# Storing a hybrid decoder's output by whole 128-partition banks, the last one in two column halves

## The chip, the core and the metric

The kernel runs on one core of a Trainium2 chip, as one program. The metric is the device time of one execution in microseconds (us). On the core, TensorE (PE in the profile) multiplies matrices into PSUM, the accumulator memory; VectorE (DVE) and ScalarE (ACT) do elementwise work; GpSimd (POOL) does small things; SyncE (SP) only issues transfers. Transfers between SBUF, the on-chip memory of 128 partitions, and DRAM run on 16 DMA engines. SP and ACT each have a queue from which these engines are fed (q1 and q10 in the profile).

## The reference

Two layers over a sequence of 256 tokens of 1024 numbers. Each layer adds half a SwiGLU block, a token mixer (a diagonal state-space mixer in layer 0, block attention in layer 1), and another half of a SwiGLU block:

```python
def swiglu(h, w_gate, w_up, w_down):
    return (jax.nn.silu(h @ w_gate) * (h @ w_up)) @ w_down
...
    for layer in range(DEPTH):
        h = h + MACARON_WEIGHT * swiglu(rms_norm(h, ffn_norm[layer, 0]), ...)
        hn = rms_norm(h, mix_norm[layer])
        ...
        h = h + MACARON_WEIGHT * swiglu(rms_norm(h, ffn_norm[layer, 1]), ...)
    return h
```

All is float32. D_MODEL is 1024, D_FF is 2816, and the output is 256 x 1024 floats, 1 MB.

## The kernel before

The residual h stays in SBUF all the time, as one tile of 128 partitions x 2 x 1024. `h[t]` is its half for tokens 128 t to 128 t + 127. Tokens are interleaved over the partitions: partition p of half t holds token 128 t + 4 (p mod 32) + p // 32. So 32 neighbouring partitions hold every fourth token, and `rows(t, s, n)` gives the DRAM list for the partitions 32 s to 32 s + 31: 32 entries, 4 rows of D = 1024 floats apart, of 512 floats each.

Weights arrive as 1 MB tiles through the SP queue. They are split into a high and a low part (`Stream.split`), and each product is made of three matmuls (`mm3`: high x high, high x low, low x high), for accuracy. All six phases run one behind the other with TensorE as the common thread. The order of the instructions on every engine is the order of the program's text.

The change touches the end of the last phase, f11, a SwiGLU block in `ffn_w`. Its second product, act @ w_down, collects in four PSUM banks `acc[2 * t + n]`: t is the half of the tokens, n the half of the 1024 columns; a bank has 128 partitions x 512 floats. `boundary` (line 362) closes every phase. For the last one (`nxt` is None) the order of the banks is (0, 0), (0, 1), (1, 0), (1, 1), called banks 0 to 3 here. Its `parts` are the last three of the 22 steps of the contraction: for each bank, three calls of `bank_mm` (line 406) with three matmuls of 512 columns each (lines 386 to 388). The parts of banks 0 and 1 but the last come first; then, bank by bank:

- the last part of banks 0 and 1, or all three parts of banks 2 and 3, on TensorE;
- `finish` (line 358): h = 0.5 * acc + h for the bank, one VectorE instruction of 512 columns (line 360);
- `store` (line 414): four transfers of 32 partitions x 512 floats, 64 KB each, the first and third from SP, the second and fourth from ACT (line 418).

Nothing else follows on TensorE and VectorE. On SP, the last weight tile has been issued long before; on ACT the last activation stands ahead of the first store. The program ends when the last transfer has landed, with waits, drains and clearing of semaphores on all engines (line 1428 in the profile).

Of the kernel before, what the change touches and what calls it, by code (L numbers as in the profile page):

```python
# [13 lines left out]
OP = mybir.AluOpType  # L14
AX = mybir.AxisListType

D = 1024
# [98 lines left out]
def trunk_kernel(ctx: ExitStack, tc, x, ffn_norm, ffn_w_gate, ffn_w_up, ffn_w_down, mix_norm,  # L116
                 s5_w_in, s5_a_re, s5_a_im, s5_log_dt, s5_b_re, s5_b_im, s5_c_re, s5_c_im, s5_d,
                 s5_w_glu, s5_w_out, moba_w_qkv, moba_q_norm, moba_k_norm, moba_w_out,
                 consts, out, phases=("f00", "s5", "f01", "f10", "moba", "f11")):
    nc = tc.nc  # L120
# [10 lines left out]
    def psM():  # L131
        return pp.tile([128, 512], F32, name="pM", tag="M", bufs=2)
# [4 lines left out]
    def psA(i):  # L137
        return pp.tile([128, 512], F32, name=f"pA{i}", tag=f"A{i}", bufs=1)

    mm = nc.tensor.matmul  # L140
# [10 lines left out]
    where = {}  # L151
# [74 lines left out]
    def warm(func):  # L226

        w = sp.tile([128, 1], F32, name="warm", tag="warm", bufs=1)
        nc.scalar.activation(w, ones[:, 0:1], func)
# [10 lines left out]
    h = [h2[:, t, :] for t in range(2)]  # L240

    def rows(t, s, n):

        tiles = [[128 * D, 2]] if t is None else []
        return [((t or 0) * 128 + s) * D + n * 512, [[4 * D, 32]] + tiles + [[1, 512]]]
# [66 lines left out]
    def prep(t, n, ph, sq=True):  # L312

        if (ph, "x") not in X:
            X.clear()
            X[ph, "x"] = True
            X["h"], X["l"] = home(XP[0], ph)
        hh = h[t][:, n * 512:(n + 1) * 512]
        ps = psR()
        pv = ps.rearrange("p (k c) -> p k c", c=128)  # L320
        for k in range(4):
            nc.tensor.transpose(pv[:, k, :], hh[:, k * 128:(k + 1) * 128], ident)  # L322
        xh, xl = (X[p][:, n * 4:n * 4 + 4, t * 128:t * 128 + 128] for p in "hl")
        nc.scalar.activation(xh, pv, AF.Copy)
        nc.vector.tensor_tensor(xl, pv, xh.bitcast(F32), op=OP.subtract)
        if sq:
            squares(t, n)
# [30 lines left out]
    def finish(t, n, acc, scale):  # L358
        hh = h[t][:, n * 512:(n + 1) * 512]
        nc.vector.scalar_tensor_tensor(hh, acc, scale, hh, op0=OP.mult, op1=OP.add)  # L360

    def boundary(nxt, parts, acc, scale, mid=None):

        if nxt is not None and nxt[0] == "f":
            order = [(0, 0), (1, 0), (0, 1), (1, 1)]
        else:
            order = [(0, 0), (0, 1), (1, 0), (1, 1)]
        for i in range(2):
            for part in parts[:-1]:
                part(*order[i])  # L370
            if mid is not None and i == 0:
                mid()
        for i, (t, n) in enumerate(order):
            for part in parts[-1:] if i < 2 else parts:
                part(t, n)
            finish(t, n, acc[2 * t + n], scale)
            if nxt is None:
                store(t, n)
            elif i:
                prep(*order[i - 1], nxt)  # L380

    def entry_hooks(ph):
        return {2: [lambda: prep(1, 1, ph)]}

    def mm3(o, xh, xl, wh, wl, start, stop):
        mm(o, xh, wh, start=start, stop=False)  # L386
        mm(o, xh, wl, start=False, stop=False)  # L387
        mm(o, xl, wh, start=False, stop=stop)  # L388

    def product(o, t, uA, uB, hooks, pumps=(1, 5)):  # L390

# [11 lines left out]
                if t == 1:  # L403
                    st.release(u, (k % 4) // 2)

    def bank_mm(acc, t, n, lh, ll, u, kks, first, last):

        for kk in kks:
            wh, wl = st.get(u, kk)
            c = slice(n * 512, n * 512 + 512)  # L410
            mm3(acc[2 * t + n], lh[:, kk, t * 128:t * 128 + 128], ll[:, kk, t * 128:t * 128 + 128],
                wh[:, c], wl[:, c], first and kk == kks[0], last and kk == kks[-1])

    def store(t, n):
        hh = h[t][:, n * 512:(n + 1) * 512]
        for s in range(4):
            off, ap = rows(t, s, n)
            (nc.sync, nc.scalar)[s % 2].dma_start(bass.AP(tensor=out.tensor, offset=out.offset + off, ap=ap),
                                                  hh[s * 32:s * 32 + 32])


    def ffn(tag, nxt, hooks, fill):
# [67 lines left out]
        def dn(j, f):  # L490
            u = where[tag, "d", j]
            for t in range(2):
                for n in range(2):
                    if j == 0 and f == 0:
                        acc[2 * t + n] = psA(2 * t + n)
                    bank_mm(acc, t, n, *AT[j], u, [f], j == 0 and f == 0, False)
                    fill(0.7)
                if t == 1:
                    st.release(u, f)
                st.pump()  # L500
# [21 lines left out]
    def ffn_w(tag, nxt, entry):  # L522

        V = nc.vector
        acc = [None] * 4
        AT = {}

        def gu(j, f, hooks):
            us = [where[tag, "g", j, a] for a in range(2)]
            ps = psM()  # L530
            for k in range(8):
                for fn in hooks.get(k, ()):
                    fn()
                wh, wl = st.get(us[k // 4], (k % 4) // 2)
                xh, xl = X["h"][:, k, :], X["l"][:, k, :]
                for i in range(2):
                    c = (k % 2) * 512 + i * 256 + f * 128
                    o = ps[:, i * 256:(i + 1) * 256]
                    a, b = wh[:, c:c + 128], wl[:, c:c + 128]
                    mm(o, a, xh, start=k == 0 and i == 0, stop=False, skip_group_check=True)  # L540
                    mm(o, a, xl, start=False, stop=False, skip_group_check=True)  # L541
                    mm(o, b, xh, start=False, stop=k == 7, skip_group_check=True)  # L542
                if k % 2:
                    if k < 7 and (j, f, k) not in ((0, 0, 1), (L, 1, 5)):
                        st.pump()
                    if f == 1:
                        st.release(us[k // 4], (k % 4) // 2)
            return ps

        def act(j, f, ps):  # L550
            gr = fp.tile([128, 2, 256], F32, name="gr", bufs=2)
            V.tensor_tensor(gr, ps.rearrange("p (i c) -> p i c", i=2),  # L552
                            Rr["row"][:, None, :].to_broadcast([128, 2, 256]), op=OP.mult)
            sg = fp.tile([128, 256], F32, name="sg", bufs=1)
            nc.scalar.activation(sg, gr[:, 0, :], AF.Silu)  # L555
            if (j, f) != (L, 1):
                st.pump()
            a = fp.tile([128, 256], F32, name="act", bufs=2)
            V.tensor_tensor(a, gr[:, 1, :], sg, op=OP.mult)
            if f == 0:  # L560
                AT[j] = []
                for i, n in enumerate(("ah", "al")):
                    o = AO[2 * i + j % 2]
                    a2 = fp.tile([128, 640], F32R, name=n, bufs=2)
                    AT[j].append(a2[:, o:o + 512].rearrange("p (f c) -> p f c", c=256))
            ah, al = (x[:, f, :] for x in AT[j])
            nc.scalar.activation(ah, a, AF.Copy)
            V.tensor_tensor(al, a, ah.bitcast(F32), op=OP.subtract)

        def dn(j, f):  # L570
            u = where[tag, "d", j]
            for t in range(2):
                for n in range(2):
                    if j == 0 and f == 0:
                        acc[2 * t + n] = psA(2 * t + n)
                    bank_mm(acc, t, n, *AT[j], u, [f], j == 0 and f == 0, False)
                if t == 1:
                    st.release(u, f)
                st.pump()

        L = NJ - 1
        for j in range(NJ):
            if j == 0:
                hooks = {}
                for k, fn in zip((0, 0, 2, 3, 4), (lambda: None, lambda: None, diag_of_r, lambda: warm(AF.Silu), rows_of_r)):
                    hooks.setdefault(k, []).append(fn)
                p0 = gu(0, 0, entry)
                hooks[4].append(lambda: act(0, 0, p0))
                p1 = gu(0, 1, hooks)
                act(0, 1, p1)  # L590
                continue
            act(j, 0, gu(j, 0, {}))
            dn(j - 1, 0)
            act(j, 1, gu(j, 1, {}))
            if j < L:
                dn(j - 1, 1)

        def part(j, f):
            return lambda t, n: bank_mm(acc, t, n, *AT[j], where[tag, "d", j], [f], False, (j, f) == (L, 1))

        boundary(nxt, [part(L - 1, 1), part(L, 0), part(L, 1)], acc, 0.5)
        st.release(where[tag, "d", L - 1], 1)
        for i in range(2):
            st.release(where[tag, "d", L], i)
# [765 lines left out]
    first = {(1, 0): [second]}  # L1370

    for i, ph in enumerate(phases):
        nxt = phases[i + 1] if i + 1 < len(phases) else None
# [59 lines left out]
```

## Time and profile before

| | |
|---|---|
| three runs | 1010.66, 1010.75, 1007.42 us; median 1010.66 |
| the profiled execution's own time | 1010.79 us |
| its span in the profile | 1009.0 us |
| mean granted TensorE clock | 0.994 |
| TensorE busy | 996.0 us, 99% of the span |
| VectorE busy | 704.6 us, 70% |
| ScalarE busy | 574.8 us, 57% |
| first issue of an output transfer | 1000.54 us from the start |
| last sum into h | 1004.58 to 1005.27 us |

How to read the lines below. A group's line has the source line, the engine, the operation, what it writes and reads, the shape and the count; behind the bar its busy time in us, the mean ns of one, and the idle time before it. A timeline's line has the start and the duration in us; "SPq" and "ACTq" are the issues of transfers. A line of a source view has the shortest, the median and the longest duration in ns, and the first and last start. A window's line has its limits and its length, then busy time and count of PE, PEld (weight loads), DVE, ACT and POOL, the granted clock, the busy share of the 16 DMA engines and GB/s. Queue lines have packets, MB and the time of the packets as a share of 16 engines' time in the window asked for.

### The profile page before, as it was taken

To read this page: it belongs to the slowest core of one execution; us is meant where nothing else is said; L and a number is where in the kernel's file an instruction comes from. 1 tells how busy PE (TensorE), PEld (TensorE's weight loads), DVE (VectorE), ACT (ScalarE), POOL (GpSimd) and SP (SyncE) were. 2 spreads that over 40 slices of the span, in tenths; PEclk is the share of its full clock that TensorE was granted. 3 is DMA by queue.
4 is the path that set the end of the run, shared out by engine and by line. 5 is a ranking of instruction groups with operands and counts; after the bars stand their busy time and mean duration, and the time that the engine had idled before them with its cause. 6 is when DMAs were issued, how large, how long until landed. Compare 5 with 4: busy or idle time off the path is not lost.

```text
span 1009.0 us, 16573 instructions
## 1 busy us (share of the span) xinstructions
PE 996.0 (99%) x6394; PEld 892.6 (88%) x6394; DVE 704.6 (70%) x1145; ACT 574.8 (57%) x1040; POOL 165.3 (16%) x330
## 2 busy tenths in 40 slices
PE   8999999999999999999999999999999999999998
PEld 7788888888998899999989999999888899999997
DVE  4799666857968677666657766666689667766662
ACT  5566777754236556555546555553788665555551
POOL 4971222113740100000010000000342010000000
PEclk9999999999899999999999999999999999999999
DMA  8896776886736557565626765655354456656531
GB/s 249 216 295 208 253 259 210 264 317 232 260 115 189 196 186 237 167 209 168 208 85 209 236 222 170 208 168 172 116 168 139 156 174 210 221 197 206 171 125 43
DMA packets 137535, 197.59 MB, mean 196 GB/s; under 512 B 16288, under 2 KB 109040, under 8 KB 137200
## 3 DMA queue, kind: packets, MB, share of 16 engines
q1 hardware_dynamic: 133264, 183.27, 56.7%
q0 software_dynamic: 3616, 12.66, 3.2%
q8 instruction: 50, 0.82, 0.3%
q10 hardware_dynamic: 576, 0.61, 0.2%
q14 instruction: 29, 0.24, 0.1%
HBM read 182.84 MB, written 13.66 MB: 195 GB/s over the span
## 4 chain that ended last, share of the span: by engine, by line
PE 91%; DVE 3%; issue 2%; POOL 2%; ACT 1%; DMA 0%; SPq 0%; ACTq 0%; POOLq 0%; DVEq 0%
PE pM L541 12%; PE pM L540 12%; PE pM L542 12%; PE pA L387 9%; PE pA L386 9%; PE pA L388 9%; PE pM L386 5%; PE pM L387 5%; PE pM L388 5%; PE pR L322 1%; DVE wlo L82 1%; POOL qrs L295 1%; PE pR L872 1%; PE pR L1035 1%; PE pR L1034 1%
## 5 line engine op out<-in xcount | busy, mean ns | idle before, releaser
L540 PE MATMUL pM<-xa,whi 128*128 128x256 f32 x1056 | 295.7, 280 | 0.0
L541 PE MATMUL pM<-xa,whi 128*128 128x256 f32 x1056 | 294.9, 279 | 0.0
L542 PE MATMUL pM<-xa,wlo 128*128 128x256 f32 x1056 | 294.7, 279 | 0.0
L88 DVE SCALAR_TENSOR_TENSOR wlo<-raw,gT,whi 128x512 fp32r<-128x512 f32 x328 | 228.0, 748 | 70.2 <-ACT whi L87 70.0
L82 DVE TENSOR_TENSOR wlo<-raw,whi 128x1024 fp32r<-128x1024 f32 x156 | 190.7, 1237 | 55.2 <-ACT whi L81 54.0
L87 ACT ACTIVATE whi<-raw,gT 128x512 fp32r<-128x512 f32 x328 | 213.5, 711 | 19.2 <-PE pA L388 14.1
L541 PEld LDWEIGHTS pM<-xa,whi 128*128 128x128 f32 x1056 | 198.5, 188 | 2.6
L540 PEld LDWEIGHTS pM<-xa,whi 128*128 128x128 f32 x1056 | 198.5, 188 | 2.3
L542 PEld LDWEIGHTS pM<-xa,wlo 128*128 128x128 f32 x1056 | 198.5, 188 | 0.0
L81 ACT ACTIVATE whi<-raw 128x1024 fp32r<-128x1024 f32 x156 | 160.8, 1054 | 21.9 <-PE pM L541 6.3
L386 PE MATMUL pA<-whi,ah 128*128 128x512 f32 x352 | 138.8, 394 | 0.0
L387 PE MATMUL pA<-wlo,ah 128*128 128x512 f32 x352 | 137.7, 391 | 0.0
L388 PE MATMUL pA<-whi,al 128*128 128x512 f32 x352 | 137.7, 391 | 0.0
L555 ACT ACTIVATE sg<-gr 128x256 f32<-128x256 f32 x66 | 27.6, 418 | 165.5 <-DVE gr L552 165.5
L386 PE MATMUL pM<-whi,xa 128*128 128x512 f32 x288 | 120.0, 417 | 1.5 <-ACT whi L81 1.5
L387 PE MATMUL pM<-wlo,xa 128*128 128x512 f32 x288 | 113.5, 394 | 0.9 <-DVE wlo L82 0.9
L388 PE MATMUL pM<-whi,xa 128*128 128x512 f32 x288 | 113.5, 394 | 0.0
L337 POOL TENSOR_TENSOR ms<-ss 128x1 f32<-128x1 f32 x10 | 1.9, 194 | 475.9 <-ACT sq L334 475.9
L388 PEld LDWEIGHTS pA<-whi,al 128*128 128x128 f32 x352 | 66.1, 188 | 14.4
L386 PEld LDWEIGHTS pA<-whi,ah 128*128 128x128 f32 x352 | 66.2, 188 | 11.6
L387 PEld LDWEIGHTS pA<-wlo,ah 128*128 128x128 f32 x352 | 66.2, 188 | 11.3
L552 DVE TENSOR_TENSOR gr<-pM,rrow 128x512 f32<-128x512 f32 x66 | 45.5, 689 | 40.6 <-PE pM L542 40.4
(253 smaller groups left out, 1289.6 us busy)
## 6 DMA issues: line engine op xcount, KB each, us to landing
raw<-in_ffn_w_down_dram SPq DMA_DIRECT2D x44, 1024.0 KB, 5.5
raw<-in_ffn_w_gate_dram SPq DMA_DIRECT2D x80, 512.0 KB, 4.0
raw<-in_ffn_w_up_dram SPq DMA_DIRECT2D x80, 512.0 KB, 5.1
raw<-in_moba_w_qkv_dram SPq DMA_DIRECT2D x12, 1024.0 KB, 5.2
TB<-dB SPq DMA_DIRECT2D x8, 768.0 KB, 5.9
raw<-in_ffn_w_gate_dram SPq DMA_DIRECT2D x16, 256.0 KB, 4.4
raw<-in_ffn_w_up_dram SPq DMA_DIRECT2D x16, 256.0 KB, 4.6
dB<-tt POOLq DMA_DIRECT2D x16, 256.0 KB, 5.2
```

What stands on the lines that cost most here:

```text
L81: nc.scalar.activation(hi, r, AF.Copy)
L82: nc.vector.tensor_tensor(lo, r, hi.bitcast(F32), op=OP.subtract)
L87: nc.scalar.activation(hi[:, c], r[:, c], AF.Identity, scale=g)
L88: nc.vector.scalar_tensor_tensor(lo[:, c], r[:, c], g, hi[:, c].bitcast(F32), op0=OP.mult, op1=OP.subtract)
L386: mm(o, xh, wh, start=start, stop=False)
L387: mm(o, xh, wl, start=False, stop=False)
L388: mm(o, xl, wh, start=False, stop=stop)
L540: mm(o, a, xh, start=k == 0 and i == 0, stop=False, skip_group_check=True)
L541: mm(o, a, xl, start=False, stop=False, skip_group_check=True)
L542: mm(o, b, xh, start=False, stop=k == 7, skip_group_check=True)
L552: V.tensor_tensor(gr, ps.rearrange("p (i c) -> p i c", i=2), Rr["row"][:, None, :].to_broadcast([128, 2, 256]), op=OP.mult)
L555: nc.scalar.activation(sg, gr[:, 0, :], AF.Silu)
```

## The change

`store` no longer issues four transfers of 32 partitions. It issues one of all 128 partitions, with a DRAM list of three dimensions: 4 entries one row apart, 32 entries four rows apart, n floats. Bank 0 goes out from SP, bank 1 from ACT, bank 2 from SP. For bank 3, the first two parts run as before. The last part runs by column halves: three matmuls of 256 columns, the sum of these 256 columns into h, and their transfer from SP; then the same for the other 256 columns, from ACT. `bank_mm` and `mm3` get the parameters for that; `skip_group_check` concerns the building of the program.

```diff
         for i, (t, n) in enumerate(order):
+            if nxt is None and i == 3:
+                for part in parts[:-1]:
+                    part(t, n)
+                for c in (0, 256):
+                    parts[-1](t, n, c)
+                    hh = h[t][:, n * 512 + c:n * 512 + c + 256]
+                    nc.vector.scalar_tensor_tensor(hh, acc[2 * t + n][:, c:c + 256], scale, hh, op0=OP.mult, op1=OP.add)
+                    store(t, n * 512 + c, 256, (nc.sync, nc.scalar)[c // 256])
+                continue
             for part in parts[-1:] if i < 2 else parts:
                 part(t, n)
             finish(t, n, acc[2 * t + n], scale)
             if nxt is None:
-                store(t, n)
+                store(t, n * 512, 512, (nc.sync, nc.scalar)[i % 2])
...
-    def mm3(o, xh, xl, wh, wl, start, stop):
-        mm(o, xh, wh, start=start, stop=False)
...
+    def mm3(o, xh, xl, wh, wl, start, stop, **kw):
+        mm(o, xh, wh, start=start, stop=False, **kw)
...
-    def bank_mm(acc, t, n, lh, ll, u, kks, first, last):
+    def bank_mm(acc, t, n, lh, ll, u, kks, first, last, half=None):
 
         for kk in kks:
             wh, wl = st.get(u, kk)
-            c = slice(n * 512, n * 512 + 512)
-            mm3(acc[2 * t + n], lh[:, kk, t * 128:t * 128 + 128], ll[:, kk, t * 128:t * 128 + 128],
-                wh[:, c], wl[:, c], first and kk == kks[0], last and kk == kks[-1])
-
-    def store(t, n):
-        hh = h[t][:, n * 512:(n + 1) * 512]
-        for s in range(4):
-            off, ap = rows(t, s, n)
-            (nc.sync, nc.scalar)[s % 2].dma_start(bass.AP(tensor=out.tensor, offset=out.offset + off, ap=ap),
-                                                  hh[s * 32:s * 32 + 32])
+            c = slice(n * 512, n * 512 + 512) if half is None else slice(n * 512 + half, n * 512 + half + 256)
+            o = acc[2 * t + n] if half is None else acc[2 * t + n][:, half:half + 256]
+            mm3(o, lh[:, kk, t * 128:t * 128 + 128], ll[:, kk, t * 128:t * 128 + 128],
+                wh[:, c], wl[:, c], first and kk == kks[0], last and kk == kks[-1], skip_group_check=(t, n) == (1, 1))
+
+    def store(t, c, n, q):
+
+        q.dma_start(bass.AP(tensor=out.tensor, offset=out.offset + t * 128 * D + c, ap=[[D, 4], [4 * D, 32], [1, n]]),
+                    h[t][:, c:c + n])
...
         def part(j, f):
-            return lambda t, n: bank_mm(acc, t, n, *AT[j], where[tag, "d", j], [f], False, (j, f) == (L, 1))
+            return lambda t, n, half=None: bank_mm(acc, t, n, *AT[j], where[tag, "d", j], [f], False, (j, f) == (L, 1), half)
```

More of the change, by code (lines that the diff above doesn't have):

```diff
@@ L383, in entry_hooks @@
         return {2: [lambda: prep(1, 1, ph)]}
-    def mm3(o, xh, xl, wh, wl, start, stop):
-        mm(o, xh, wh, start=start, stop=False)
-        mm(o, xh, wl, start=False, stop=False)
-        mm(o, xl, wh, start=False, stop=stop)
+    def mm3(o, xh, xl, wh, wl, start, stop, **kw):
+        mm(o, xh, wh, start=start, stop=False, **kw)
+        mm(o, xh, wl, start=False, stop=False, **kw)
+        mm(o, xl, wh, start=False, stop=stop, **kw)
     def product(o, t, uA, uB, hooks, pumps=(1, 5)):
```

## The prediction

> **What bounds the kernel now.** I read the page first, for its span, its chain and its queues.
>
> ```profile
> span 1009.0 us, 16573 instructions
> PE 996.0 (99%) x6394; PEld 892.6 (88%) x6394; DVE 704.6 (70%) x1145; ACT 574.8 (57%) x1040; POOL 165.3 (16%) x330
> ...
> q1 hardware_dynamic: 133264, 183.27, 56.7%
> ...
> PE 91%; DVE 3%; issue 2%; POOL 2%; ACT 1%; DMA 0%; SPq 0%; ACTq 0%; POOLq 0%; DVEq 0%
> ...
> out_dram<-h SPq DMA_DIRECT2D x8, 64.0 KB, 1.8
> out_dram<-h ACTq DMA_DIRECT2D x8, 64.0 KB, 2.0
> ```
>
> TensorE bounds the kernel from end to end, and the diff leaves its work untouched up to the last three products. So only the tail can change: the time from the first output transfer to the end. The timeline shows it, with start and duration in us.
>
> ```profile
> 1000.54 5.54 SPq L418 DMA_DIRECT2D out_dram<-h  x8
> 1000.55 5.61 ACTq L418 DMA_DIRECT2D out_dram<-h  x8
> ...
> 1003.70 0.39 PE L386 MATMUL pA<-whi,ah 128*128 128x512 f32 x1
> ...
> 1003.93 0.39 PE L387 MATMUL pA<-wlo,ah 128*128 128x512 f32 x1
> ...
> 1004.16 0.39 PE L388 MATMUL pA<-whi,al 128*128 128x512 f32 x1
> 1004.58 0.69 DVE L360 SCALAR_TENSOR_TENSOR h<-pA,h 128x512 f32<-128x512 f32 x1 [1.35 <-PE pA L388]
> ```
>
> The last product ends near 1004.55, the last sum at 1004.58 + 0.69 = 1005.27, and then nothing but transfers is left. Windows of 0.2 us (the last two columns are the busy share of 16 DMA engines and GB/s) show when bytes move.
>
> ```profile
> 1001.20:1001.40 0.20, 0.20 (x2) 0.19 (x1) 0.00 (x0) 0.00 (x0) 0.00 (x0) 1.00 0.04 10
> 1001.40:1001.60 0.20, 0.20 (x2) 0.16 (x1) 0.00 (x0) 0.00 (x0) 0.00 (x0) 1.00 1.03 246
> ...
> 1006.20:1006.40 0.20, 0.00 (x0) 0.00 (x0) 0.00 (x0) 0.00 (x0) 0.00 (x0) 1.00 0.85 205
> ...
> 1006.80:1007.00 0.20, 0.00 (x0) 0.00 (x0) 0.00 (x0) 0.00 (x0) 0.00 (x0) 1.00 1.11 349
> 1007.00:1007.20 0.20, 0.00 (x0) 0.00 (x0) 0.00 (x0) 0.00 (x0) 0.00 (x0) 0.93 0.79 184
> 1007.20:1007.40 0.20, 0.00 (x0) 0.00 (x0) 0.00 (x0) 0.00 (x0) 0.00 (x0) 0.50 0.07 10
> ```
>
> The first issue is at 1000.54 and the first bytes move at 1001.4: 0.86 us to start. The last bytes move at 1007.3, and the span ends at 1009.0: 1.7 us of closing, which no edit touches. The slack in this tail is small: after 1005.27 there are 2.0 us until the last byte, and 0.86 of them are the start.
>
> **How many engines carry a transfer.** This decides the case. The view of the queues, over 980 to 1012 us, counts packets of the output alone (two are instruction fetches).
>
> ```profile
> DMA packets 770, 1.07 MB, mean 34 GB/s; under 512 B 256, under 2 KB 256, under 8 KB 768
> ...
> q10 hardware_dynamic: 384, 0.52, 6.8%
> q1 hardware_dynamic: 384, 0.52, 5.6%
> ```
>
> Sixteen transfers of 32 rows give 512 packets of 2 KB. The other 256 are small: 16 for each transfer, which I read as one completion mark from each of 16 engines. Each of these transfers has an outermost count of 32 on both sides, and 32 deals out evenly to 16 engines. Every other list of the kernel begins with 16, 32, 128 or 256. The changed store is the first that does not: its SBUF side begins with 128 partitions, but its DRAM side is [[D, 4], [4D, 32], [1, n]] and begins with 4. If entries of the outermost count are dealt to the engines, 4 entries reach 4 engines at most.
>
> No row of before shows a transfer on fewer than 16 engines, so I bound the cost from both sides: 16 engines as now, or 4. I take 4, because 16 marks with counts of 32 fit dealing by the outermost count, and one count of 4 can't be dealt to 16. The Trainium skill states this as a rule (DMA: Bandwidth & Descriptors, "Why a DMA increments its semaphore by 16 and not by 1"): the number of engines is the largest one up to 16 that divides the slowest dimension larger than 1 of both sides, so 128 against 4 gives 4. The 16 marks per transfer agree with it for 32 against 32; no run here shows it for 4. By the rule the time is the forecast below, and by the rows alone, which know only 16, it would be the first rival's.
>
> **The parts of the change.**
>
> *Issues.* Sixteen issues become five: bank 0 on SP, bank 1 on ACT, bank 2 on SP, and the halves of bank 3 on SP and ACT. Their two lists differ in shape. The nearest row is the load of TE (its lists begin with 256 and 128 entries), against TA with equal lists.
>
> ```profile
> L943 SPq DMA_DIRECT2D TE<-dE x8: 529/530/617, 214.5 to 271.5; - x8
> ...
> L939 SPq DMA_DIRECT2D TA<-dA x8: 319/401/600, 214.1 to 263.7; - x8
> ...
> L418 SPq DMA_DIRECT2D out_dram<-h x8: 314/389/424, 1000.5 to 1005.7; - x8
> L418 ACTq DMA_DIRECT2D out_dram<-h x8: 374/434/446, 1000.5 to 1005.7; - x8
> ```
>
> An issue then takes 0.53 instead of 0.39 us, so the first bytes come at 1001.4 + 0.14, about 1001.5. At the very end one issue of 0.53 per queue replaces two of 0.39 to 0.43: a gain of 0.3 us there, counted only where the issue, not the engines, ends last. ACT and SP have nothing behind these issues but the closing.
>
> *Products, sums and a new wait.* Three products of 512 columns become six of 256. PE's pitch for the two widths, and VectorE's time for a sum of 512 and for the same operation out of PSUM at 256:
>
> ```profile
> 990.59 0.28 PE L540 MATMUL pM<-xa,whi 128*128 128x256 f32 x1
> ...
> 990.71 0.28 PE L541 MATMUL pM<-xa,whi 128*128 128x256 f32 x1
> ```
> ```profile
> L360 DVE SCALAR_TENSOR_TENSOR h<-pA,h 128x512 f32<-128x512 f32 x24 | 16.5, 692 | 17.6 <-PE pA L388 17.6
> ...
> L472 DVE SCALAR_TENSOR_TENSOR act<-pM,rr,sg 128x256 f32<-128x256 f32 x20 | 9.6, 478 | 6.7 <-ACT sg L468 6.7
> ```
>
> Six at 0.12 cost what three at 0.23 do. But in the built program the first product of the second half waits for the sum of the first half, because both use one PSUM bank. So PE and VectorE take turns: the first half's products start at 1003.70, its third at 1003.94, ending 0.28 later at 1004.22; sum until 1004.24 + 0.48 = 1004.72; the second half's products from 1004.75 to 1004.75 + 0.24 + 0.28 = 1005.27; sum until 1005.77. The last sum ends 0.5 us later than before. Behind the waiting product stand only two more on PE; for them wait the last sum and the last issue on ACT. With 4 engines this costs nothing, since the engines still have bytes to move for 8.8 us by then (below); with 16 it shows.
>
> *Bytes.* Four banks of 128 x 512 floats are 1.049 MB. On 4 engines that is 0.262 MB for each. What does a busy engine move? The fastest stretch of the loads bounds it from one side: over 213 to 272 us, slices with a share of 9 tenths or more reach 429 GB/s.
>
> ```profile
> DMA  0599999999999559389427471505999719999992
> GB/s 11 133 340 296 352 385 421 413 429 419 396 411 415 214 169 422 136 122 425 169 67 278 89 289 19 162 0 72 414 408 389 319 15 281 403 346 410 400 389 83
> ```
>
> 429 / 16 = 26.8 GB/s for an engine, so 0.262 MB take 9.8 us. From the other side: the outputs on q10 moved 0.52 MB in 6.8% of 16 x 32 us = 34.8 engine-us, 15 GB/s, so 17.5 us. The page's q1 over the whole run lies between: 183.27 MB in 56.7% of 16 x 1009 us = 9154 engine-us, 20.0 GB/s, so 13.1 us. The best window of the outputs agrees: 349 GB/s at a share of 1.11 is 19.7 GB/s for each busy engine. I take 20.0.
>
> The four engines never run dry: by 1001.5 bank 0 is there, bank 1 is issued at about 1001.2, bank 2 at 1003.2 (the sum that ends then), the halves of bank 3 at 1004.7 and 1005.8, and by 1005.8 the engines have done 4.3 of 13.1 us.
>
> **The sum**, against the profiled execution: bytes end at 1001.5 + 13.1 = 1014.6; closing 1.7; span 1016.3. That execution took 1010.79 with a span of 1009.0, so 1.8 lies around it: 1018.1. It stands 0.1 above the median of the three runs (1010.66), so I forecast 1018.0, slower by 7.3 us or 0.7%. With 26.8 GB/s it is 1014.8, with 15 GB/s 1022.5.
>
> **The rivals.**
>
> *All 16 engines carry the new transfers: no change.* For it: nothing in the trace shows a transfer on fewer, and the larger side has 128 entries. Against it: the count of 4. Then the wait decides: last sum at 1005.77, one issue, bytes from 1005.78 + 0.14 + 0.86 = 1006.78, 0.131 MB on 16 engines at 20 GB/s 0.4 us, end of bytes 1007.2 instead of 1007.3. The gain at the issues and the loss at the wait cancel: 1010.6.
>
> *Faster ports.* The same 16 engines, but now at the loads' rate: the outputs moved 205 GB/s at a share of 0.85, 15 for a busy engine, where the loads reach 26.8. If reading 32 partitions at a time is what slows them, reading 128 brings the last half out in 0.3 instead of 0.4 us, and the time is 1010.5. The Trainium skill (SBUF — State Buffer, "Door 1: The DMA port swizzle") says just this, that 32 neighbouring partitions reach half of the ports. The slow rows agree; the gain is a tenth of a us, because the start and the closing stay.
>
> *Four engines that get in each other's way.* Each then reads a block of 32 partitions, and neighbours share what limits 32-partition reads today. This is the 15 GB/s bound: 1022.5.
>
> *One engine*, if lists of unequal shape aren't dealt out at all: 1.049 MB at 20 GB/s are 52 us, 1057. The load of TE speaks against it: 4.0 us for 260 KB is far too fast for that.
>
> **How the numbers follow.** Four engines: 0.78, of it 0.10 for the 15 GB/s end. Sixteen, with or without faster reads: 0.19. One engine or anything else: 0.03. A measurement of this kernel can tell about 0.5%, 5.05 us, from no change. The bound lies at 1015.7, where an engine would move 24.5 GB/s: above what the outputs ever show, under the best loads. So of the 0.78, 0.69 are slower and 0.09 the same; of the 0.19, 0.18 are the same and 0.01 faster; of the 0.03, 0.02 slower and 0.01 faster. Together faster 0.02, same 0.27, slower 0.71. The likeliest case's own range is 1014.8 to 1022.5. It leaves out more than 2 in 10, so the range goes down past the second case, to 1010.3, and ends at 1021.5.
>
> **What would show it.** Right: the small packets of the output fall from 256 to 5 x 4 = 20 (80 with 16 engines); the windows after 1002 show a share near 0.25 and 60 to 100 GB/s for 10 us or more; PE's last products are as early as before, with a gap of about 0.5 us between the halves; issues last 0.5 us. Wrong: 80 small packets, or bytes that end before 1008.

## The result, and the profile after

The changed kernel took 1015.83 us (median of nine runs, 1012.84 to 1017.03), the kernel before 1010.66 us in the same rounds (nine runs, 1007.42 to 1011.99). The ratio is 1.0054, with a 95% interval of 1.0039 to 1.0069: slower by about 5.2 us. A second measurement on another occasion (e5 below) gave 1.0082 (1.0067 to 1.0096). Single executions of the kernel before lay between 1006.0 and 1012.4 us, as far apart as the effect itself. A part of this scatter shows in the traces: some executions of either kernel run at half the TensorE clock for about 3.4 us near 28 us from their start and for about 6.8 us near 270 us. How often that fell on either side in the two measurements is a likely reason for their difference, but only one execution of each run was profiled. The profiles below are therefore compared by their tails: a tail is the time from the first issue of an output to the end of the span.

The page of the changed kernel, and its timeline at the end (start and duration in us):

```profile
span 1011.1 us, 16564 instructions
...
PE 990.6 (98%) x6397; PEld 888.0 (88%) x6397; DVE 706.4 (70%) x1146; ACT 574.6 (57%) x1040; POOL 165.5 (16%) x330
```
```profile
995.64 4.69 SPq L426 DMA_DIRECT2D out_dram<-h  x3
```
```profile
996.32 5.17 ACTq L426 DMA_DIRECT2D out_dram<-h  x2
```
```profile
998.80 0.28 PE L395 MATMUL pA<-whi,ah 128*128 128x256 f32 x1
...
998.91 0.28 PE L396 MATMUL pA<-wlo,ah 128*128 128x256 f32 x1
...
999.03 0.28 PE L397 MATMUL pA<-whi,al 128*128 128x256 f32 x1
999.35 0.42 DVE L380 SCALAR_TENSOR_TENSOR h<-pA,h 128x256 f32<-128x256 f32 x1 [1.01 <-PE pA L397]
...
999.83 0.39 PE L395 MATMUL pA<-whi,ah 128*128 128x256 f32 x1 [0.52 <-DVE h L380]
...
1000.05 0.28 PE L396 MATMUL pA<-wlo,ah 128*128 128x256 f32 x1
...
1000.17 0.28 PE L397 MATMUL pA<-whi,al 128*128 128x256 f32 x1
1000.49 0.42 DVE L380 SCALAR_TENSOR_TENSOR h<-pA,h 128x256 f32<-128x256 f32 x1 [0.71 <-PE pA L397]
```

This execution reached its first output issue at 995.64, 4.9 us earlier than the profiled one of before. It had neither stretch of half clock. In windows around them (the column before the last two is the granted clock), before stands first, the changed kernel second:

```profile
25.00:33.00 8.00, 6.04 (x19) 4.57 (x20) 4.78 (x6) 4.64 (x7) 6.87 (x15) 0.79 0.71 172
268.00:278.00 10.00, 8.90 (x50) 8.69 (x50) 8.98 (x17) 2.29 (x5) 7.65 (x7) 0.66 0.60 210
```
```profile
25.00:33.00 8.00, 5.98 (x26) 4.44 (x27) 6.44 (x7) 5.61 (x8) 7.19 (x11) 1.00 0.76 175
268.00:278.00 10.00, 10.00 (x90) 10.00 (x90) 9.65 (x16) 2.29 (x5) 8.48 (x8) 1.00 0.49 167
```

A mean of 0.79 over 8 us is half clock for 3.4 us, and 0.66 over 10 us is half clock for 6.8 us; from 28 to 30 and from 270 to 276 us the trace of before has 0.50. The other profiled executions bear this out. Those with neither stretch (changed, e4, e7) reach their first output issue at 995.6 to 996.1 us, those with both (before, e1, e2, e3, e5, e9) at 999.9 to 1000.5.

The tail itself went from 1009.0 - 1000.54 = 8.5 us to 1011.1 - 995.64 = 15.4 us. VectorE is done at 1000.49 + 0.42 = 1000.91; what follows for ten microseconds is only the transfers. The view of the queues over 980 to 1020 us shows them (a row of 40 slices, then packets and queues), and so do windows of the tail:

```profile
GB/s 0 0 0 0 8 16 0 0 0 0 0 0 0 0 0 0 6 25 37 78 104 98 96 90 101 97 100 96 87 32 0 0 0 0 0 0 0 0 0 0
DMA packets 662, 1.07 MB, mean 27 GB/s; under 512 B 20, under 2 KB 276, under 8 KB 660
...
q1 hardware_dynamic: 396, 0.66, 5.4%
q10 hardware_dynamic: 264, 0.39, 2.6%
```
```profile
996.50:997.00 0.50, 0.50 (x4) 0.39 (x3) 0.00 (x0) 0.00 (x0) 0.00 (x0) 1.00 0.04 12
997.00:997.50 0.50, 0.50 (x4) 0.42 (x3) 0.00 (x0) 0.00 (x0) 0.00 (x0) 1.00 0.39 37
997.50:998.00 0.50, 0.50 (x4) 0.42 (x3) 0.36 (x1) 0.00 (x0) 0.00 (x0) 1.00 0.28 12
998.00:998.50 0.50, 0.50 (x4) 0.42 (x3) 0.33 (x1) 0.00 (x0) 0.00 (x0) 1.00 0.06 8
...
1005.00:1006.00 1.00, 0.00 (x0) 0.00 (x0) 0.00 (x0) 0.00 (x0) 0.00 (x0) 0.50 0.25 97
```

What SP waits for at the end (us in total, times, longest), the changed kernel first, then before:

```profile
SPq L1436 <- DMA out_dram<-h: 9.3, 4, 4.8
```
```profile
SPq L1428 <- DMA out_dram<-h: 1.5, 1, 1.5
```

Five transfers leave 20 small packets, four for each, where before sixteen left 256. The engines' share is 0.25, a quarter of 16, and four engines move 97 GB/s, 24 each. SP waits 9.3 us for landings, before 1.5 us.

### The profile page after: what moved, and what is told of

Same layout as the page of the kernel before. It is cut to its first block, busy times and chain, and to the rows that moved or that the text cites. A ratio compares the mean times of both kernels' runs of the same rounds, so it can differ in the third digit from the quotient of the medians.

```text
span 1011.1 us, 16564 instructions
## 1 busy us (share of the span) xinstructions
PE 990.6 (98%) x6397; PEld 888.0 (88%) x6397; DVE 706.4 (70%) x1146; ACT 574.6 (57%) x1040; POOL 165.5 (16%) x330
## 4 chain that ended last, share of the span: by engine, by line
PE 89%; DVE 3%; issue 2%; POOL 2%; ACT 2%; DMA 1%; SPq 0%; ACTq 0%; POOLq 0%; DVEq 0%
PE pM L549 12%; PE pM L548 12%; PE pM L550 12%; PE pA L396 9%; PE pA L395 9%; PE pA L397 9%; PE pM L395 5%; PE pM L396 5%; PE pM L397 5%; PE pR L322 1%; POOL qrs L295 1%; DVE wlo L82 1%; PE pR L880 1%; PE pR L1042 1%; PE pR L1043 1%
```

## The experiments

The theory: a store runs on as many engines as its DRAM list has outermost entries, up to 16; here that is four, and they are the whole cost. The rivals: the column halves with their wait, the unequal lists as such, or something ahead of the tail. The table has all runs; the time of the first issue, of the first and last byte and of the end are from the one profiled execution of each run. With the lists of e1, e4, e6, e7, e9 and e10 the rows land in another order than the reference's, so these kernels serve only to measure.

| run | outermost entries | halves | small packets | first byte after first issue, us | last byte after first issue, us | tail, us |
|---|---|---|---|---|---|---|
| before | 32 (four transfers a bank) | no | 256 | 0.85 | 6.78 | 8.47 |
| changed | 4 | yes | 20 | 1.27 | 14.05 | 15.41 |
| e5, changed again | 4 | yes | 20 | 1.27 | 14.02 | 15.38 |
| e2 | 4 | no | 16 | 1.27 | 14.02 | 15.38 |
| e1 | 16 | yes | 80 | 1.27 | 7.24 | 8.57 |
| e4 | 16 | no | 64 | 1.27 | 7.26 | 8.64 |
| e3 | 32 (four transfers a bank) | yes | 256 | 0.85 | 7.31 | 9.00 |
| e6 | 2 | yes | 10 | 1.24 | 23.31 | 24.68 |
| e7 | 8 | yes | 40 | 1.33 | 7.97 | 9.30 |
| e8 | 32, other pairs | no | 256 | 0.86 | 6.74 | 8.56 |
| e9 | 128, equal lists | yes | 80 | 0.85 | 6.67 | 8.00 |
| e10 | 128, equal lists | no | 64 | 0.85 | 6.49 | 7.87 |

**e1: sixteen outermost entries.**

```diff
-        q.dma_start(bass.AP(tensor=out.tensor, offset=out.offset + t * 128 * D + c, ap=[[D, 4], [4 * D, 32], [1, n]]),
+        q.dma_start(bass.AP(tensor=out.tensor, offset=out.offset + t * 128 * D + c, ap=[[D, 16], [16 * D, 8], [1, n]]),
```

> The changed kernel with one edit: the DRAM list of a store begins with 16 entries instead of 4 ([[D, 16], [16 D, 8], [1, n]]), so the rows leave in another order than the reference's; sizes, queues, halves and unequal lists stay. Tail = first issue of an output to the end of the span; it was 8.5 us before and 15.5 us after. Theory (the outermost count sets the number of engines): 5 x 16 = 80 small packets, tail 8.3 to 9.2 us, time some 6 us below the changed kernel's in the same rounds and within 1 us of the kernel before, apart from the spread of single runs. Rival (unequal lists, the larger transfers or the wait between the halves cost the time): tail stays above 14 us.

Measured: ratio to before 1.0004 (0.999 to 1.0018). The queue view over 990 to 1022 us:

```profile
DMA packets 720, 1.05 MB, mean 33 GB/s; under 512 B 80, under 2 KB 336, under 8 KB 720
```

80 small packets, 16 for a transfer, and the tail is back at 8.57 us, 0.1 us above before. The list is the whole loss, since nothing else was changed. The order of the rows in DRAM changes with it; that the count is what matters is shown by e6 and e7 below, whose shares of the engines follow it.

**e2: no halves.** The lines added in `boundary` for bank 3 are taken out again, so bank 3 goes the way of the others.

```diff
-            if nxt is None and i == 3:
...
-                continue
             for part in parts[-1:] if i < 2 else parts:
```

> The changed kernel without the column halves: bank 3 has its products at 512 columns, one sum and one store of 256 KB with the list that begins with 4. Theory: the four engines are busy from 1.3 us after the first issue to the end, so the halves and their wait are hidden: tail 15.5 us, within 0.3 of the changed kernel, 20 - 4 = 16 small packets. Rival (the halves cost the time): tail 8.5 to 9.5 us.

Measured: tail 15.38 against 15.41, 16 small packets; ratio 1.0082 (1.0062 to 1.0103), where the changed kernel in its second measurement has the same 1.0082. With four engines the halves are neither the cost nor a help: their wait is hidden behind the transfers.

**e3: the halves alone**, in the kernel before, with its old stores after the second sum.

```diff
+            if nxt is None and i == 3:
+                for part in parts[:-1]:
+                    part(t, n)
+                for c in (0, 256):
+                    parts[-1](t, n, c)
+                    hh = h[t][:, n * 512 + c:n * 512 + c + 256]
+                    nc.vector.scalar_tensor_tensor(hh, acc[2 * t + n][:, c:c + 256], scale, hh, op0=OP.mult, op1=OP.add)
+                store(t, n)
+                continue
```

> The kernel before with the column halves alone: last part of bank 3 in two halves with the wait and two sums, then the old four stores of 32 partitions. Theory: last sum 0.3 to 0.5 us later against the products, tail 8.9 us, 256 small packets, time +0.4 us, not to be told from before by time. Rival (the halves cost the time): tail 12 us or more.

Measured: ratio 0.9999 (0.9984 to 1.0014), tail 9.00 us, 0.53 more than before and a little above the 8.9 expected. The timeline of the run shows the price of the wait where nothing hides it:

```profile
1003.31 0.28 PE L395 MATMUL pA<-whi,ah 128*128 128x256 f32 x1
...
1003.86 0.42 DVE L380 SCALAR_TENSOR_TENSOR h<-pA,h 128x256 f32<-128x256 f32 x1 [1.01 <-PE pA L397]
...
1004.34 0.38 PE L395 MATMUL pA<-whi,ah 128*128 128x256 f32 x1 [0.52 <-DVE h L380]
...
1004.99 0.42 DVE L380 SCALAR_TENSOR_TENSOR h<-pA,h 128x256 f32<-128x256 f32 x1 [0.71 <-PE pA L397]
```

PE and VectorE take turns; the last sum ends 1.13 us after the first one does.

**e4: sixteen entries and no halves**, the edits of e1 and e2 together.

> The changed kernel without halves and with the list that begins with 16 (rows in another order than the reference's): whole-bank transfers on 16 engines and nothing else. Theory: 64 small packets; one issue at the end instead of two, packets at 84 ns instead of 145, so tail 8.0 to 8.4 us, a gain of 0.1 to 0.5 us against before that time alone can't show. Rival (reading 128 partitions at once is slower): tail above 9 us.

Measured: tail 8.64 us, neither the gain of the theory nor the loss of the rival; ratio 0.9997 (0.9982 to 1.0012). Together with e1 it says that with these lists and 16 engines the halves are worth nothing: 8.57 with, 8.64 without. The last issue comes 0.54 us later with the halves (5.30 against 4.76 us after the first), but it carries half the bytes, and the last byte lands at the same time. With the equal lists of e9 and e10 below the halves cost 0.13 us.

**e5: the changed kernel again.**

> The changed kernel once more, beside the kernel before on one chip. In the first measurement its median was 5.2 us above, but its tail was 6.9 us longer (15.4 against 8.5). Theory (the tail is the whole cost; the rest is how often an execution drops to half clock for 3.4 us at 28 us and 6.8 us at 270 us, which is chance): with more runs the median difference goes to 6.9 +- 0.8 us and the tail stays 15.4. Rival (the change also shortens something ahead of the tail by 1.7 us): the difference stays at 5.2.

Measured: 1017.48 us against 1009.44, ratio 1.0082 (1.0067 to 1.0096), so 8.0 us by medians, and a tail of 15.38 us. The difference of medians is on the other side of 6.9 this time, by 1.1: beyond the 0.8 of the expectation, which is missed, and further still from the 5.2 of the rival. All six runs had a mean clock of 0.990 or 0.991, and the profiled one of them had both stretches of half clock; of the 17 runs of before, three were at 0.999 or 1.000 and took 1006.0 to 1006.2 us. Over all measurements, 15 runs of the changed kernel have a median of 1016.2, and 55 of before (9, 29 and 17) one of 1009.8: 6.4 us. The tail repeats to 0.03 us, the medians to a few us.

**e6 and e7: two and eight entries.**

```diff
+        q.dma_start(bass.AP(tensor=out.tensor, offset=out.offset + t * 128 * D + c, ap=[[D, 2], [2 * D, 64], [1, n]]),
```
```diff
+        q.dma_start(bass.AP(tensor=out.tensor, offset=out.offset + t * 128 * D + c, ap=[[D, 8], [8 * D, 16], [1, n]]),
```

> The changed kernel with a list that begins with 2 ([[D, 2], [2 D, 64], [1, n]]; rows in another order than the reference's). Theory (engines = outermost count, each at 24.5 GB/s): 5 x 2 = 10 small packets; 1.049 MB on two engines take 21.4 us; with 1.3 to the first byte, up to 1 of slow start and 1.4 of closing the tail is 24.1 to 25.1 us. Rival (the unequal list costs a fixed time whatever its count): tail 15.4.

> The changed kernel with a list that begins with 8 ([[D, 8], [8 D, 16], [1, n]]; rows in another order than the reference's). Theory: 40 small packets; 8 engines move a bank in 1.3 us, faster than the banks come, so the last half decides: issued 5.3 us after the first, 1.3 to the first byte, 0.7 for 128 KB, 1.4 closing: tail 8.7 to 9.3 us. Rival (a fixed cost of the unequal list): tail 15.4.

Measured: tails of 24.68 and 9.30 us, 10 and 40 small packets. Windows of e6, then of e7:

```profile
1010.00:1015.00 5.00, 0.00 (x0) 0.00 (x0) 0.00 (x0) 0.00 (x0) 0.00 (x0) 0.50 0.13 50
```
```profile
999.00:1001.00 2.00, 0.86 (x6) 0.46 (x4) 0.85 (x2) 0.00 (x0) 0.00 (x0) 1.00 0.54 185
```

The share is 2/16 and 8/16, and the rate 25 and 23 GB/s for an engine. The tail follows the count: 24.7, 15.4, 9.3, 8.6 us for 2, 4, 8 and 16. With eight the engines nearly keep up with the banks, and the gain of the next doubling is small.

**e8: other pairs of blocks** in the kernel before.

```diff
-            (nc.sync, nc.scalar)[s % 2].dma_start(bass.AP(tensor=out.tensor, offset=out.offset + off, ap=ap),
+            (nc.sync, nc.scalar)[s // 2].dma_start(bass.AP(tensor=out.tensor, offset=out.offset + off, ap=ap),
```

> The kernel before with one edit: SP issues the stores of partitions 0-31 and 32-63, ACT those of 64-95 and 96-127 (before: 0-31 and 64-95, 32-63 and 96-127), so that the two transfers in flight at once read from different halves of the partitions. Theory of ports (the 145 ns packets of before are two neighbouring blocks of 32 sharing ports): the mean 2 KB packet falls from 120 towards 84 ns, the last byte comes 0.2 to 0.4 us earlier, tail 8.1 to 8.3 us. Rival (one block of 32 partitions on 16 engines already crowds its ports by itself): mean stays above 110 ns, tail 8.4 to 8.6. Time alone can't tell either.

Measured: mean packet 114 ns, tail 8.56 us, ratio 1.0005 (0.9989 to 1.0021): the rival's numbers, though not its mechanism, as the blocks of the upper half show. The queue view over 990 to 1008 us splits the mean:

```profile
q1 hardware_dynamic: 384, 0.52, 13.1%
q10 hardware_dynamic: 384, 0.52, 7.9%
```

The same bytes cost q1, which reads partitions 0 to 63, 1.7 times the engine time of q10, which reads 64 to 127. In the trace q10's packets take 84 ns nearly all, q1's about 145. So the pairing moves the slow packets to one queue, and that queue ends as late as before. A block of 32 partitions on 16 engines isn't slow as such.

**e9 and e10: equal lists**, 128 rows in the order of the partitions, with halves and without.

```diff
+        q.dma_start(bass.AP(tensor=out.tensor, offset=out.offset + t * 128 * D + c, ap=[[D, 128], [1, n]]),
```

> The changed kernel with stores whose two lists are equal: 128 rows in the order of the partitions ([[D, 128], [1, n]]; another order than the reference's). With a list that begins with 16 the first byte came 1.27 us after the first issue, against 0.85 before, and an issue took 0.53 us or more. Theory (the unequal lists cost this): first byte at 0.85 us, issues of 0.4 us, 80 small packets, tail 8.0 to 8.2 us (8.57 - 0.42). Rival (the size of a transfer, 128 entries instead of 32, costs it): first byte at 1.27, tail 8.5 to 8.6.

> The same equal lists with whole banks and no halves (rows in another order than the reference's). Theory: the tail of the list that begins with 16 was 8.64 us with whole banks; less 0.42 it is 8.2 us, with issues of 0.4 us and 64 small packets: at best 0.3 us below the kernel before, so that no layout of these stores is worth more. Rival (first byte at 1.27 whatever the list): 8.6 us.

Measured: tails 8.00 and 7.87 us, 80 and 64 small packets, first byte at 0.85. The source view of the store in e9, after it that of e1:

```profile
L426 SPq DMA_DIRECT2D out_dram<-h x3: 332/356/357, 999.9 to 1004.0; - x3
L426 ACTq DMA_DIRECT2D out_dram<-h x2: 351/358/366, 1000.6 to 1005.2; - x2
```
```profile
L426 SPq DMA_DIRECT2D out_dram<-h x3: 538/570/607, 1000.0 to 1004.1; - x3
L426 ACTq DMA_DIRECT2D out_dram<-h x2: 555/602/650, 1000.7 to 1005.3; - x2
```

Unequal lists cost 0.2 us more at each issue and 0.42 us more to the first byte; before, with equal lists and rows four apart, has the same 0.85 us as e9, so the order of the rows isn't what costs this. And e9's 2 KB packets take 86 ns in the mean, where e1's take 114 and before's 120: a window of e9 moved 420 GB/s. So e9 lies at the lower end of what was expected, and e10 0.3 us below its 8.2, which fits packets that became faster too. Whether the faster packets come from the equal lists or from the new order of the rows in DRAM no run separates. The two together would be worth 0.5 to 0.6 us of the tail, but with this layout of the tokens the rows would land in the wrong places, so no version that beats the kernel before came out of it.

## Why the prediction was right

- *Four engines.* Right: 20 small packets and a share of 0.25. It was the step with no row of its own, and the runs with 2, 4, 8 and 16 entries show it for this store. The Trainium skill's rule (DMA: Bandwidth & Descriptors, "Why a DMA increments its semaphore by 16 and not by 1") said it beforehand, and the four counts agree with it.
- *The bytes.* 13.1 us forecast, 14.05 - 1.27 = 12.8 measured, but not at the even 20.0 GB/s of the sum. In the slices from 1000 to 1009 us the four engines moved 87 to 104 GB/s, 22 to 26 each, near the upper bound. 1.049 MB at 4 x 24.5 GB/s would be 10.7 us. The trace has only 0.076 MB moved 3.5 us after the first issue, where 98 GB/s from the first byte on would have needed 0.8 of the 2.2 us: so about 1.5 of the missing 2.1 us are lost at the start, and the rest later. The mean over the whole run that stood for the rate came out right by luck: it was too low for the steady part and knew nothing of the slow start. The forecast's 15 GB/s bound fell: steady packets of 2 KB take 84 ns, 24 GB/s.
- *The first byte.* 0.14 us later, said the row of TE's issue; it was 0.42. This term was mis-sized: the longer issue is not the only thing that unequal lists delay. The issues themselves took 0.53 to 0.67 us on SP and 0.55 on ACT, near the 0.53 forecast, but ACT's first took 1.15. The start at 1001.5 in the sum would have been 1001.8.
- *Closing.* 1.7 us forecast as untouchable, 1.36 measured, and 1.33 to 1.38 in every run with four or five output transfers against 1.69 to 1.82 with sixteen. It offsets the first byte's error.
- *The wait.* The last sum ends 5.27 us after the first issue instead of 4.73: 0.54 later, forecast 0.5. That it costs nothing beside four engines is shown by e2, and that it costs 0.53 without them by e3.
- *The sum.* The tail grew by 6.9 us, forecast 7.3. The median of the first measurement says 5.2, of the second 8.0. The sum was made against one execution and left out what varies ahead of the tail, the half-clock stretches above all.
- *The rivals.* Sixteen engines: fell, though its price was right: e1, which has them, takes as long as before. Faster ports: fell too. A tail of 7.9 or 8.0 instead of 8.5 us was there to be had, more than the 0.1 us of the working, but only with equal lists and their other order of rows; e1 and e4, which also read 128 partitions at once, have 8.57 and 8.64. The reading behind this rival, that 32 partitions at a time are slow, fits only some blocks: in e8 those of the upper half took 84 ns a packet. Four engines in each other's way: fell, by the same 84 ns. One engine: fell.

## What to carry to other kernels

Before a transfer is made larger, look at the outermost count of both its lists: 128 partitions on one side don't help when the other side begins with 4. Here the small packets per transfer in the queue view showed at once how many engines carried it. When single executions differ by as much as the effect, and the change touches only a tail in which nothing else runs, compare the tails of the traces and not the medians.

## What the runs had that was not expected

- A slow start on few engines. In the windows above, four engines moved 37, 12 and 8 GB/s in the first one and a half microseconds, and 97 from 1005 to 1006 us. In the trace the third to sixteenth packets of the first transfer, by their start, take 144 to 940 ns each; the same pattern is in e2 and e5, and a weaker one in e6 and e7 (up to 389 and 514 ns). In these five runs ACT's first issue takes 1.13 to 1.21 us, with 16 entries 0.65. No run here tells what they wait for.
- Packets of 2 KB took about 145 ns from partitions 0 to 63 and 84 ns from 64 to 127 in e8, and 86 ns in the mean with equal lists of 128. But in e8 each half has a queue of its own, and the halves alone don't explain before: there SP's packets from 64 to 95 take 84 ns in three of four banks, but ACT's from 96 to 127 in the same banks take 129 to 137, right behind the slow ones from 32 to 63 (means by transfer, with the packets of a queue counted off in the order of issue). What makes the packets slow is open.
- Closing is 0.3 to 0.5 us shorter with four or five transfers than with sixteen; which of the closing waits it is was not tried.
